# All low parts of the mixing stages' weights on VectorE

## The chip, the cores and the metric

The kernel runs on one core of one Trainium2 chip. The metric is the device time of one execution in microseconds (us); lower is better. The kernel before took 2455.51 us, the median of 3 runs (2453.41 to 2462.34).

## The reference

Two transformer blocks one after the other on x, 512 tokens of 1024 features in float32. What matters here is the order of the stages and which weights each multiplies:

```python
def hybrid_layer(...):                                  # first block
    x = x + 0.5 * swiglu_ffn(rmsnorm(x, ffn1_norm_g), ffn1_w_in, ffn1_w_out)
    h = rmsnorm(x, mix_norm_g)
    # h @ w_in -> q, k, v, conv and gates; block attention + gated convolution + memory attention
    x = x + (g_nsa * o_nsa + g_conv * o_conv + g_mem * o_mem) @ w_out
    x = x + 0.5 * swiglu_ffn(rmsnorm(x, ffn2_norm_g), ffn2_w_in, ffn2_w_out)

def second_block(...):
    x = x + _mixer_block(_rms(x, norm_mix_w), w_in, ...)  # windowed attention + gated linear attention
    x = x + _memory_xattn(_rms(x, norm_mem_q_w), _rms(mem, norm_mem_kv_w), ...)
    x = x + _swiglu(_rms(x, norm_ffn_w), w_gate, w_up, w_down)
    return _rms(x, norm_final_w)
```

Every `@` with a weight is a float32 product that the kernel makes of three products of shorter numbers.

## The kernel before

The stages follow each other: feed-forward f1, mixing stage `mix1`, feed-forward f2, mixing stage `mix2` with the memory attention `xattn` behind it, feed-forward f3. x is kept transposed, as 8 tiles of 128 features x 512 tokens.

A number is split into a high part (rounded to the matmul's input type) and a low part (what the rounding left). `mm3` (L233) multiplies high by high, high by low and low by high, so each weight has to be there as a pair `wh`, `wl`. `w` (L268 on) makes the pair: a DMA brings 128x1024 raw numbers into a tile `wr` (three buffers), ScalarE rounds them (`copy`, the CAST of L260, into `wh`), and then one `tensor_tensor` subtracts `wh` from `wr` into `wl` (all of them carry L242, the line of the helper `tt`). `wh` and `wl` have three buffers each in the mixing stages, so a pair can be made while the two before it are in use or ready. Both inputs of the subtraction lie in SBUF.

Which engine subtracts is said by the list `self.wes`, through which `w` goes round by a running number. In the feed-forward stages it is `[nc.vector]`; before `mix1` and before `mix2` it is set to `[nc.gpsimd, nc.gpsimd, nc.vector]`, so there two of three low parts are made by GpSimd and one by VectorE. `xattn` follows `mix2` with the same list. The 199 weight tiles of `mix1`, `mix2` and `xattn` give 133 subtractions to GpSimd. Two halves in `setup` are on GpSimd by name (`split=True`) and have nothing to do with the list.

Besides that, GpSimd multiplies and adds 128x512 tiles in the mixing stages (`cv`, `x`: L242 as well): 40 instructions. VectorE has most of what else is neither matmul nor activation: it evacuates each 512-column product from PSUM (`chunk` returns to a `mul` or `stt` by the caller), makes the low parts of activations (`split`, `stack`), the minima and scalings of the softmaxes, the recurrence `st` of the linear attention and the square roots (`rsqrt`). Some of these instructions read PSUM and one tile of SBUF, some read two tiles of SBUF: in `softmax_mem` the small `nm<-nm,mr4y` (128x1), in `nsa_v` the low part `vt<-vtmp,vt`, in `gla` the gate `og<-sq,og`, in `rsqrt` all its steps.

The code sets the order of the calls, but the framework sorts each engine's instructions by its own estimate of when they can start and puts in all waits; on the chip each engine then works its list off in that order. A low part made on VectorE therefore stands at some place of VectorE's list that the code alone doesn't tell; on GpSimd it stands in a list of its own.

Of the kernel before, what the change touches and what calls it, by code (L numbers as in the profile page):

```python
# [204 lines left out]
class _Net:  # L205
# [1662 lines left out]
    def run(self):  # L1868
        nc, tc = self.nc, self.tc
        self.PSB = {"g": 3, "s": 2, "t": 2, "o": 1}  # L1870
        self.pi = 0
        self.todo = []
        self.pre = {}
        self.mid, self.half = None, 3
        self.wes = [nc.vector]
        with ExitStack() as es:
            self.g = es.enter_context(tc.tile_pool(name="glob", bufs=1))
            self.wps = [(es.enter_context(tc.tile_pool(name="wts", bufs=1)), WC, 3)]
            self.wi = self.wk = 0
            self.pp = es.enter_context(tc.tile_pool(name="psum", bufs=1, space=bass.MemoryType.PSUM))  # L1880
            dp = es.enter_context(tc.tile_pool(name="dram", bufs=1, space=bass.MemoryType.DRAM))
            self.xd = dp.tile([KT, P, S], F32, name="xd")
            self.drel = dp.tile([16, LINE], F32, name="drel")
            self.dcmp = dp.tile([16, 1024], F32, name="dcmp")
            self.setup()
            self.gl5 = self.t(self.g, [P, 2], F32, "gl5", 1)
            o = _OFF["glan"]
            self.ts(self.gl5, self.cols[:, o:o + 2], 0.5, ALU.mult)
            self.oneb = self.ones[:, 0:1]

            def step(key, spill, late=False):
                self.begin_norm(key)

                def hook(n):
                    if spill:
                        self.spill(n)
                    self.norm_x(n)
                    if not late:
                        self.norm_sq(n)

                self.hook = hook
                return hook

            def done(tag):
                if tag in self.dbg:
                    for j in range(KT):
                        nc.sync.dma_start(self.dbg[tag][j], self.X[j])

            self.xq = es.enter_context(self.pool("xq", "right"))
            self.open_u()  # L1910
            step("ffn1", False)
            for j in range(KT):
                self.norm_x(j)
            for j in range(KT):
                self.norm_sq(j)
            self.end_norm()

            self.mem = {}

            def memory():  # L1920
                self.memkeep, self.memtmp = ExitStack(), ExitStack()
                keep = self.memkeep.enter_context(self.pool("memkeep", "right"))
                tmp = self.memtmp.enter_context(self.pool("memtmp", "right"))
                prep = self.mem_prep(tmp, keep, "mem1", "memn", self.mem, True)
                tabs = self.tables(tmp)
                self.todo = prep[:9] + tabs[:1] + prep[9:] + tabs[1:]

            self.ffn("f1", 0.5, self.deferred(step, "mix", True), 3, memory)
            self.memtmp.close()
            self.upool.__exit__(None, None, None)  # L1930
            done("d_f1")
            self.end_norm()
            self.pending("ffn2", False, step)
            self.wes = [nc.gpsimd, nc.gpsimd, nc.vector]
            self.mix1()
            self.wes = [nc.vector]
            done("d_m1")
            self.end_norm()
            self.ffn("f2", 0.5, self.deferred(step, "mix2", True), 3)
            self.upool.__exit__(None, None, None)  # L1940
            done("d_f2")
            self.end_norm()
            self.pending("mq2", False, step)
            self.wes = [nc.gpsimd, nc.gpsimd, nc.vector]
            self.mix2()
            done("d_m2")
            self.end_norm()
            self.pending("ffn3", False, step, True)
            self.xattn()
            self.xpool.__exit__(None, None, None)  # L1950
            self.wes = [nc.vector]
            done("d_x2")
            self.end_norm()
            self.open_u()
            self.ffn("f3", 1.0, None, 3)
            self.upool.__exit__(None, None, None)
# [33 lines left out]
```

## Time and profile before

| what | before |
|---|---|
| median of 3 runs | 2455.51 us (2453.41 to 2462.34) |
| the profiled execution | 2457.26 us; its span, first to last instruction, 2455.5 us |
| TensorE (PE) busy | 2365.4 us, 96% of the span |
| weight loads (PEld) busy | 2048.3 us, 83% |
| VectorE (DVE) busy | 1710.2 us, 70% |
| ScalarE (ACT) busy | 1160.2 us, 47% |
| GpSimd (POOL) busy | 431.6 us, 18% |
| low parts on GpSimd (`wl`) | 135 instructions, 317.2 us |
| low parts on VectorE (`wl<-wr,wh`) | 270 instructions, 326.5 us |

An engine's busy time is what it executes, waiting included where an instruction has started and can't go on; idle time has a releaser, the work whose end let the engine go on. PEclk is the granted clock of TensorE, 1.00 for 2.4 GHz and 0.50 for 1.2 GHz. The stages lie about so: f1 to 340 us, `mix1` 340 to 1140, f2 to 1480, `mix2` and `xattn` 1480 to 2060, f3 to the end.

### The profile page before, as it was taken

How to read it: one execution, taken by the hardware profiler on the slowest of the kernel's cores; microseconds unless marked ns; L12 is line 12 of the kernel's file. 1: busy time of each engine (PE TensorE's matmuls, PEld its weight loads, DVE VectorE, ACT ScalarE, POOL GpSimd, SP SyncE). 2: the span in 40 equal slices, each digit the busy share in tenths (PEclk: the TensorE clock that was granted, in tenths of full speed). 3: DMA queues.
4: the chain of work that ended last, by engine and by line, in shares of the span. 5: the costliest groups of instructions: out<-in, count | busy, mean ns of one | idle time of the engine just before them, and what ended most of it. 6: DMA issues, size and time to landing. Idle time of an engine off the chain costs nothing.

```text
span 2455.5 us, 35462 instructions
## 1 busy us (share of the span) xinstructions
PE 2365.4 (96%) x13618; PEld 2048.3 (83%) x13618; DVE 1710.2 (70%) x3150; ACT 1160.2 (47%) x2084; POOL 431.6 (18%) x260
## 2 busy tenths in 40 slices
PE   8999999899999999999999999998999998999997
PEld 7999978687788788877989898797888886889897
DVE  7766876865668666876767675558875367867675
ACT  6534443343445544545535353554665346644353
POOL 0000014331222222231000002121122331000000
PEclk9999999999999999999999999999999998999999
DMA  6645544231222122224445453122222331555551
GB/s 191 176 129 159 148 143 151 85 113 53 74 69 73 58 87 69 69 65 163 127 153 148 140 144 122 52 86 63 69 69 71 122 125 60 150 155 142 160 141 57
DMA packets 91318, 272.14 MB, mean 111 GB/s; under 512 B 10775, under 2 KB 19001, under 8 KB 91020
## 3 DMA queue, kind: packets, MB, share of 16 engines
q1 hardware_dynamic: 82748, 239.81, 29.7%
q0 software_dynamic: 8400, 30.06, 6.8%
q8 instruction: 107, 1.75, 0.3%
q14 instruction: 63, 0.52, 0.1%
HBM read 263.44 MB, written 6.40 MB: 110 GB/s over the span
## 4 chain that ended last, share of the span: by engine, by line
PE 63%; DVE 11%; ACT 2%; issue 2%; DMA 1%; POOL 0%; DVEq 0%; ACTq 0%; POOLq 0%
PE g L231 36%; PE s L231 12%; PE t L231 10%; PE o L231 3%; PE t L239 2%; DVE wl L242 2%; ACT wh L260 1%; DVE qk L242 1%; DMA wr<-f_s 1%; DVE sp L1259 0%; DMA wr<-f_o 0%; DVE cv L254 0%; DVE o L254 0%; POOL wl L242 0%; DVE xs L242 0%
## 5 line engine op out<-in xcount | busy, mean ns | idle before, releaser
L231 PE MATMUL g<-xs,wh 128*128 128x512 f32 (+1 forms) x3064 | 900.6, 376 | 7.4 <-ACT wh L260 3.0
L260 ACT CAST wh<-wr 128x1024 fp32r<-128x1024 f32 (+6 forms) x405 | 410.3, 1016 | 574.8 <-PE g L231 219.8
L231 PEld LDWEIGHTS g<-xs,wh 128*128 128x128 f32 x3064 | 555.1, 192 | 100.1 <-ACT wh L260 3.5
L231 PE MATMUL g<-xs,wl 128*128 128x512 f32 (+1 forms) x1532 | 573.2, 374 | 6.3 <-POOL wl L242 3.6
L242 POOL TENSOR_TENSOR wl<-wr,wh 128x1024 fp32r<-128x1024 f32 (+4 forms) x135 | 317.2, 2351 | 862.3 <-ACT wh L260 684.9
L242 DVE TENSOR_TENSOR wl<-wr,wh 128x1024 fp32r<-128x1024 f32 (+6 forms) x270 | 326.5, 1211 | 69.9 <-ACT wh L260 67.4
L231 PEld LDWEIGHTS g<-xs,wl 128*128 128x128 f32 x1532 | 293.2, 191 | 58.6 <-POOL wl L242 4.9
L231 PE MATMUL s<-xs,wh 128*128 128x256 f32 (+1 forms) x876 | 219.0, 339 | 1.4 <-ACT wh L260 1.4
L231 PE MATMUL t<-xs,wh 128*128 128x512 f32 (+1 forms) x860 | 213.2, 337 | 0.1
L555 POOL DMA_DIRECT2D wr<-f_s x57 | 49.1, 861 | 849.2 <-DMA wr<-f_s 202.3
L231 PEld LDWEIGHTS s<-xs,wh 128*128 128x128 f32 x876 | 150.5, 189 | 20.8 <-ACT wh L260 2.6
L231 PEld LDWEIGHTS t<-xs,wh 128*128 128x128 f32 x860 | 147.8, 189 | 18.1 <-DVE xs L242 0.5
L231 PE MATMUL t<-xs,wl 128*128 128x512 f32 (+1 forms) x430 | 145.4, 338 | 3.7 <-DVE wl L242 3.7
L231 PE MATMUL s<-xs,wl 128*128 128x256 f32 (+1 forms) x438 | 148.2, 338 | 0.0
L257 ACT ACTIVATE sp<-sp,nm 128x128 f32<-128x128 f32 x192 | 101.9, 532 | 55.2 <-DVE nm L1259 42.4
L242 DVE TENSOR_TENSOR ptl<-t,pth 128x512 fp32r<-128x512 f32 (+1 forms) x128 | 73.5, 603 | 55.5 <-ACT pth L260 55.1
L260 ACT CAST pth<-t 128x512 fp32r<-128x512 f32 (+1 forms) x128 | 62.1, 520 | 92.7 <-PE t L239 92.1
L231 PEld LDWEIGHTS t<-xs,wl 128*128 128x128 f32 x430 | 81.2, 189 | 13.1 <-DVE wl L242 4.5
L231 PEld LDWEIGHTS s<-xs,wl 128*128 128x128 f32 x438 | 82.9, 189 | 9.0
L231 PE MATMUL g<-th,wl 128*128 128x256 f32 x292 | 82.7, 283 | 1.5 <-DVE wl L242 1.0
L231 PE MATMUL g<-tl,wh 128*128 128x256 f32 x292 | 81.5, 279 | 0.0
L231 PE MATMUL g<-th,wh 128*128 128x256 f32 x292 | 81.5, 279 | 0.0
(521 smaller groups left out, 4820.0 us busy)
## 6 DMA issues: line engine op xcount, KB each, us to landing
wr<-f_ab SPq DMA_DIRECT2D x73, 512.0 KB, 3.8
wr<-f_s SPq DMA_DIRECT2D x57, 512.0 KB, 4.8
wr<-f_s POOLq DMA_DIRECT2D x57, 512.0 KB, 6.8
wr<-f_o SPq DMA_DIRECT2D x48, 448.0 KB, 3.8
wr<-m_f SPq DMA_DIRECT2D x40, 512.0 KB, 3.7
wr<-m_o SPq DMA_DIRECT2D x40, 512.0 KB, 3.5
w<-f_ab SPq DMA_DIRECT2D x57, 256.0 KB, 4.2
wr<-f_o SPq DMA_DIRECT2D x24, 512.0 KB, 4.7
```

Of the source, the lines that this page charges most:

```text
L231: self.pm = self.nc.tensor.matmul(o, l, r, start=first, stop=last, skip_group_check=more)
L239: self.nc.tensor.transpose(o, i, self.ident)
L242: (e or self.nc.vector).tensor_tensor(o, x, y, op=op)
L257: return self.nc.scalar.activation(o, x, f, **k)
L260: return self.nc.scalar.copy(o, x)
L555: nc.gpsimd.dma_start(rs, a[key + "_s"][c][:, D:], accum_op=ALU.add)
```

## The change

Before both mixing stages the list of engines for the low parts is one engine long, VectorE. The 133 subtractions that GpSimd did there go to VectorE; the roundings, the DMAs, the buffers and the matmuls are the same, and so are the 40 other GpSimd instructions and the two halves in `setup`.

```diff
             self.pending("ffn2", False, step)
-            self.wes = [nc.gpsimd, nc.gpsimd, nc.vector]
+            self.wes = [nc.vector]
             self.mix1()
             self.wes = [nc.vector]
             done("d_m1")
...
             self.pending("mq2", False, step)
-            self.wes = [nc.gpsimd, nc.gpsimd, nc.vector]
+            self.wes = [nc.vector]
             self.mix2()
```

## Rows read from the trace of the kernel before

**Rows 1.** Busy time by stage: us, busy (instructions) per engine, clock, DMA.
```profile
340.00:1140.00 800.00, 762.69 (x3881) 626.52 (x3880) 570.54 (x1188) 358.60 (x717) 224.83 (x111) 0.97 0.27 87
1140.00:1480.00 340.00, 337.71 (x2262) 309.85 (x2261) 243.72 (x376) 160.97 (x236) 18.84 (x20) 1.00 0.50 142
1480.00:2060.00 580.00, 563.03 (x2817) 470.74 (x2815) 369.66 (x729) 287.17 (x588) 147.71 (x81) 0.99 0.26 87
```

**Rows 2.** The same for instructions with `wl` alone: PE, PEld, DVE, POOL.
```profile
340.00:1140.00 800.00, 322.61 (x852) 164.52 (x852) 53.73 (x41) 178.70 (x75) 0.97 0.27 87
1480.00:2060.00 580.00, 266.54 (x698) 132.23 (x697) 36.28 (x29) 133.46 (x57) 0.99 0.26 87
```

**Rows 3.** Durations by tile: ns min/median/max, first and last start, shapes.
```profile
L242 POOL TENSOR_TENSOR wl<-wr,wh x135: 1277/2397/3245, 9.4 to 2048.6; 128x1024 fp32r<-128x1024 f32 x117, 128x768 fp32r<-128x768 f32 x6, 128x560 fp32r<-128x560 f32 x5, 128x912 fp32r<-128x912 f32 x5
L242 DVE TENSOR_TENSOR wl<-ws,wh x57: 1215/1225/1226, 47.9 to 2385.0; 128x1024 fp32r<-128x1024 f32 x57
L242 DVE TENSOR_TENSOR nm<-nm,mr4y x16: 152/159/2158, 544.9 to 608.3; 128x1 f32<-128x1 f32 x16
```

**Rows 4.** Timeline near 563 us, by engine: start, us, instruction, [idle before <-releaser].
```profile
563.31 2.16 DVE L242 TENSOR_TENSOR nm<-nm,mr4y 128x1 f32<-128x1 f32 x1
...
563.08 2.37 POOL L242 TENSOR_TENSOR wl<-wr,wh 128x1024 fp32r<-128x1024 f32 x1 [16.26 <-ACT wh L260]
...
566.21 0.38 PE L231 MATMUL s<-kmh,qh 128*128 128x256 f32 x1 [1.75 <-ACT pm L257]
```

**Rows 5.** Timeline near 892 us.
```profile
891.79 2.30 DVE L242 TENSOR_TENSOR vt<-vtmp,vt 128x256 fp32r<-128x256 f32 x1 [0.47 <-ACT vt L260]
...
891.46 2.34 POOL L242 TENSOR_TENSOR wl<-wr,wh 128x1024 fp32r<-128x1024 f32 x1 [2.51 <-ACT wh L260]
...
894.82 0.70 PE L239 MATMUL t<-ident,tabc 128*128 128x128 f32 x4 [3.75 <-DVE tabc L242]
```

**Rows 6.** Timeline: first and last of 89 lengthened VectorE groups, x2 of both.
```profile
345.30 3.03 DVE L254 SCALAR_TENSOR_TENSOR ml<-mraw,cols,mh 128x256 fp32r<-128x256 f32 x2
...
2046.38 2.83 DVE L242 TENSOR_TENSOR q<-qr,q 64x512 fp32r<-64x512 f32 x2
```

**Rows 7.** TensorE's waits in 340 to 1140 us: total us, times, longest.
```profile
PE g L231 <- DVE wl L242: 4.8, 2, 2.7
PE t L239 <- DVE tabc L242: 4.1, 3, 3.7
PE s L231 <- ACT pm L257: 3.9, 3, 1.7
PE g L231 <- POOL wl L242: 3.6, 3, 1.7
...
PE o L231 <- DVE rsl L242: 2.4, 2, 1.8
```

**Rows 8.** TensorE's waits in 1480 to 2060 us.
```profile
PE t L231 <- DVE stl L242: 5.5, 5, 1.5
PE t L239 <- DVE x L249: 2.5, 1, 2.5
PE o L231 <- ACT rsh L260: 2.0, 1, 2.0
```

**Rows 9.** Granted clock (0.50, after PEld, DVE, ACT, POOL) right behind rows 5.
```profile
895.30:898.70 3.40, 3.40 (x12) 2.92 (x11) 3.18 (x11) 2.25 (x8) 0.00 (x0) 0.50 0.42 161
```

**Rows 10.** Chain that ended last, 340 to 1140 us: shares of the 800 us.
```profile
by line: PE g L231 39.6%; PE s L231 6.4%; PE o L231 6.3%; PE t L239 5.3%; PE t L231 3.7%; DVE qk L242 1.9%; DVE sp L1259 1.4%; DVE wl L242 1.3%; issue 1.2%; DVE cv L254 1.1%; DVE o L254 0.9%; DVE nm L242 0.8%; ACT wh L260 0.8%; DVE vt L242 
```

**Rows 11.** VectorE's idle time before its `wl`, 1480 to 2060 us, and times.
```profile
  ACT wh L260: 32.4, 12
```

**Rows 12.** Timelines near 461 us: a run of VectorE work, TensorE's wait.
```profile
460.52 1.23 DVE L242 TENSOR_TENSOR wl<-wr,wh 128x1024 fp32r<-128x1024 f32 x1
...
461.80 0.79 PE L231 MATMUL g<-xs,wl 128*128 128x512 f32 x1 [2.69 <-DVE wl L242]
...
467.50 5.10 DVE L242 TENSOR_TENSOR zr<-kcr,pe 64x256 f32<-64x256 f32 x5
```

## The prediction

> **What bounds the kernel now.** I read the busy time by stage first [rows 1]. TensorE is idle for 800 - 762.7 = 37.3 us of `mix1` and 580 - 563.0 = 17.0 us of `mix2` with `xattn`; in f2, where VectorE makes every low part already, it is idle for 2.3 of 340 us. So TensorE bounds all stages, and what can be won in the mixing stages is those 54 us and the time lost to a lower clock (mean 0.97 and 0.99, which is 24 and 6 us of full-clock work). VectorE is busy for 71% and 64% of the two stages, as in f2 (72%): it is not the bound on average, but it feeds TensorE.
>
> Then TensorE's waits by releaser [rows 7, 8]. Hardly any names a low part made by GpSimd (3.6 us). Most name VectorE, or ScalarE directly behind VectorE, and the timelines at those places show one pattern. At 563 us VectorE's `nm<-nm,mr4y`, which works on one column and mostly takes 0.16 us [rows 3], takes 2.16 us; GpSimd's subtraction started 0.23 us earlier and ends at 565.45, and the small instruction ends 0.02 us later; the matmul behind it waited 1.75 us [rows 4]. At 892 us `vt<-vtmp,vt` takes 2.30 us for 256 columns, where VectorE's subtraction of 1024 takes 1.22 [rows 3]; it ends 0.29 us behind GpSimd's, and TensorE waited 3.75 us in all, a second held one having run a little earlier [rows 5]. All lengthened instructions have two inputs in SBUF. There are 89 of them beside a low part on GpSimd between 340 and 2060 us (the first and last are in the two groups of [rows 6]); their durations less those of the same instruction without GpSimd beside it sum to 140 us: 83 in `mix1`, 55 behind it, 2 between.
>
> **Removed.** 133 subtractions leave GpSimd (75 and 57 in the two stages [rows 2], one between), and with them 312 us of its time. GpSimd isn't on the path but for the 3.6 us, so its own time is worth little. What is worth something is VectorE's 140 us. The 40 other GpSimd instructions stay, and what they lengthen (10 us in 12 cases) stays with them.
>
> How much of that does TensorE feel? I go through its waits and give each the smaller of its length and of the lengthening just ahead of it. `mix1`: `pm` 3.9 (three times the `nm` case), `tabc` 3.5 of 4.1, `rsl` 2.4, VectorE's own `wl` 2.1 of 4.8 (one of its two was itself held): 11.9 us [rows 7]. `mix2`: `stl` 5.2 of 5.5 (behind a held gate or query instruction), `x` 2.1 of 2.5 (one held square-root step), `rsh` 2.0 (the same): 9.3 us [rows 8]. A dozen others of 0.3 to 2.0 us each give 10, as far as all of them together stay under the 54 us of idle time [rows 1]. Sum 31 us. Where one is lifted, ScalarE's link or the next evacuation is late next; I keep four fifths, 25 us, with 15 (half) and 31 as ends.
>
> The waits for a GpSimd `wl` (3.6 us) are for an instruction of 2.40 us that becomes one of 1.22 us [rows 3]: 1.8 us, ends 0 and 3.6.
>
> **Clock.** Behind such waits the granted clock falls to 0.50 (1.2 GHz) for a while: right behind the 3.75 us wait it is 0.50 for 3.4 us [rows 9]. I find six such stretches, from 366 to 2028 us, directly behind a wait of the list above, 34 us long together, in which 17 us of full-clock work were lost. Some have other waits beside them that stay: I take 8 us, ends 0 and 17.
>
> **Added.** VectorE gets 117 subtractions of 1024 columns at 1.225 us [rows 3], 143 us, and 16 narrower ones which, scaled by columns, make about 14: 158 us. It gives up 138 in the two stages, so its load there goes from 940 to some 960 of 1380 us [rows 1], 68 to 70%. It doesn't saturate. Were nothing lifted it would be 1098 us, 80%.
>
> What a subtraction costs depends on where it stands in VectorE's list, which the trace of before doesn't show for the 133. Two bounds. Below: nothing, if it falls into VectorE's idle 30%; a pair can be made two weight tiles ahead, so its own lateness has slack. A gain beyond the lifted waits is excluded, since the work is added. Above: the full 1.22 us whenever VectorE is on the path. The nearest rows are VectorE's own subtractions in the same stages: in `mix1` they hold 1.3% of the chain, 10.4 us [rows 10], of which 2.1 was the held one, so 8.3 us for 41, 0.20 each. In `mix2` they lie under the lines that the chain's row shows, 1.2 us for 29. 76 x 0.20 + 57 x 0.04 = 17.5 us on the chain. Some 41 us of VectorE's lengthening lay on the chain and came to the 31 us at TensorE, so I take three quarters of the 17.5 and a little for the fuller queue: +15 us, ends 0 and 38 (the whole of the compression's price below).
>
> One new wait: the subtraction waits at the head of VectorE's list for ScalarE's cast, with all evacuations queued behind it. VectorE's own 29 in `mix2` idled 32.4 us so, 12 times [rows 11], and no wait of TensorE there names them [rows 8]; I put it into the 15.
>
> **Sum.** -25 - 1.8 - 8 + 15 = -20 us, against the profiled execution's 2457.3 us: 2437.5. That execution lies 1.8 us over the median of the runs, so 2436 as a median.
>
> **Rivals.** (a) The delay is only exchanged. The subtraction can start where it starts today, when the cast is done; if it then stands ahead of the same `nm`, `vt` or `og`, it holds them for 1.22 us. 158 us come, 138 go, and the waits grow in that ratio, 31 x 158 / 138 = 35.5: with the 1.8 us back, 2455 + 2.7 = 2458; if the clock stretches shorten somewhat, 2450. For it: today's GpSimd subtractions are released by the same casts. Against it: the framework can put a VectorE subtraction behind a short instruction that is ready, and the 70 already there cost 0.20 and 0.04 us, not 1.22.
>
> (b) Slower: low parts come late in the compression of `mix1`. There VectorE runs `zr` for 5.10 us in one piece, and a subtraction on VectorE behind three `zr` has made TensorE wait 2.69 us [rows 12]. Between 450 and 550 us GpSimd makes 14 low parts. At 2.7 us each that is 38 us; the other 119 at 0.12 each (4.8 us for 41 [rows 2, 7]) make 14. With 25 + 2 + 8 lifted: 2455 + 17 = 2472. It decides from the point where a moved subtraction costs TensorE more than 35 / 133 = 0.26 us on average. For it: the run of 5.10 us. Against: 20 of the 140 us of lengthening lie between 450 and 550 us, and go. The Trainium skill, "Perfetto Trace Analysis", Optimizing Scalar/DVE Operations, says that where VectorE is saturated, handing work to ScalarE or even GpSimd may make sense. By that rule alone the change undoes a sensible split and (b) would hold. The same place adds that moving work between those two might not help since they share a read port of SBUF, and the held instructions of [rows 4, 5] agree with this second half.
>
> (c) It changes nothing, because few instructions move: excluded by the list's length, as all 199 tiles take its one entry.
>
> **Chances.** Forecast (2424 to 2446) 0.60, (a) (2442 to 2464) 0.26, (b) (2460 to 2490) 0.14. A measurement here tells about 0.5% from no change, 12.3 us, which is under 2443.2 or over 2467.8. Of the forecast 0.55 lies below 2443, 0.05 above; of (a) 0.02 is faster, 0.23 same, 0.01 slower, since it rests on a ratio; of (b) 0.02 same, 0.12 slower. So faster 0.57, same 0.30, slower 0.13. The range leaves out a tenth at each side: 2418 (the sum with 31 lifted, 3.6 for the late low parts, 8 for the clock and 3 added comes to 2416) to 2471 (the foot of (b)).
>
> **What would show it.** Right: VectorE's `nm<-nm,mr4y` has its longest under 0.5 us, `vt`, `og`, `qgl` and the square-root steps likewise; GpSimd's busy time falls to about 120 us; VectorE's stays within 30 us of 1710; TensorE's waits on `pm`, `tabc`, `stl`, `rsh` shrink to under half, and its idle time in the two stages from 54 to some 40 us or less; fewer stretches at 1.2 GHz. Wrong by (a): the same waits, now behind a 1.22 us `wl` on VectorE. Wrong by (b): waits `g <- DVE wl` of 2 us and more between 440 and 530 us. Wrong altogether would be VectorE's instructions still held to 2.4 us, by the 40 that stay.

## The result: 2398.8 us, and the profile after

| | before | after |
|---|---|---|
| median of the runs shown | 2455.59 us | 2398.80 us (2397.29 to 2403.09) |
| ratio to before, 95% interval | | 0.9767 [0.9748, 0.9785] |
| profiled execution | 2457.26 us | 2403.09 us |
| its span | 2455.5 us | 2401.0 us |
| mean granted clock | 0.980 | 0.989 |
| VectorE busy | 1710.2 us | 1720.8 us |
| GpSimd busy | 431.6 us | 119.8 us |

The change gains 57 us by the medians and 54 us between the two profiled executions. The forecast was 20 us, the fast end of its range 2418. So the direction was right, and the gain lies 19 us outside the range.

The busy time by stage, the first three columns being the stretch, its length and TensorE's busy time, then TensorE's weight loads, VectorE, ScalarE, GpSimd, clock and DMA. The stretches begin and end at the same TensorE instructions as those of [rows 1], to within a few of them:

```profile
340.00:1100.00 760.00, 747.28 (x3876) 615.43 (x3875) 566.27 (x1260) 357.32 (x715) 47.24 (x36) 0.99 0.29 91
1100.00:1440.00 340.00, 338.08 (x2263) 310.28 (x2262) 243.39 (x377) 161.03 (x236) 17.92 (x24) 1.00 0.51 142
1440.00:2006.00 566.00, 559.71 (x2819) 467.26 (x2817) 385.01 (x790) 287.76 (x591) 14.31 (x19) 1.00 0.28 89
```

Against [rows 1], `mix1` went from 800 to 760 us and `mix2` with `xattn` from 580 to 566: 40 and 14 us, the whole 54. The stage between them, f2, kept its 340. TensorE's idle time fell from 37.3 to 12.7 us and from 17.0 to 6.3, together from 54.3 to 19.0. The clock's mean rose from 0.97 and 0.99 to 0.99 and 1.00. Before, the records hold eight stretches at 1.2 GHz in `mix1`, 44 us long; after, these two parts of 6.8 us each (the second begins at 1070 us), of which this is the first:

```profile
507.00:513.80 6.80, 6.80 (x22) 5.53 (x22) 3.24 (x14) 1.14 (x2) 0.00 (x0) 0.50 0.21 72
```

In the second part there were two, 13.6 us long, and a third began 0.8 us before its end; after, one is left, which begins 4 us before the end. So 58.8 us at 1.2 GHz became 17.6, eleven stretches became three, and half of the difference, some 20 us, is full-clock work won back. Idle time gives 35 us and the clock 20, together the 54 us to within 2 us.

The instructions that make or read `wl` alone, same columns:

```profile
340.00:1100.00 760.00, 318.42 (x850) 161.16 (x851) 138.25 (x116) 0.00 (x0) 0.99 0.29 91
1440.00:2006.00 566.00, 264.90 (x698) 131.01 (x697) 109.23 (x86) 0.00 (x0) 1.00 0.28 89
```

Where [rows 2] has 41 and 29 subtractions on VectorE and 75 and 57 on GpSimd, all 116 and 86 are now on VectorE. VectorE got 84.5 + 73.0 = 158 us of work, as forecast, and yet is busy for 566 us as against 571 in `mix1` and 385 as against 370 behind it. The rest was time in which its instructions had been held. That is seen in their durations (ns, least, median and greatest):

```profile
L242 DVE TENSOR_TENSOR nm<-nm,mr4y x16: 151/159/161, 525.4 to 583.6; 128x1 f32<-128x1 f32 x16
L242 DVE TENSOR_TENSOR vt<-vtmp,vt x8: 411/418/426, 622.5 to 861.8; 128x256 fp32r<-128x256 f32 x8
```

`nm<-nm,mr4y` had a longest of 2158 ns [rows 3] and the `vt` of [rows 5] took 2.30 us. Now the longest of each is within 2% of its median. TensorE's waits in 340 to 1100 us (total, times, longest), for [rows 7]:

```profile
PE g L231 <- DVE wl L242: 3.1, 3, 1.5
PE t L239 <- DVE sp L249: 2.4, 6, 0.8
PE g L231 <- ACT xs L260: 2.0, 1, 2.0
PE o L231 <- DVE ptl L242: 1.6, 3, 0.6
...
PE s L231 <- DVE nm L1259: 0.7, 4, 0.2
PE t L239 <- DVE tabc L242: 0.4, 2, 0.2
```

`pm` and `rsl` have gone, `tabc` has 0.4 of its 4.1 us left, and `wl` on VectorE 3.1 of 4.8, though it is now made 116 times instead of 41. In `mix2`, for [rows 8]:

```profile
PE s L231 <- ACT pm L257: 1.2, 3, 0.7
PE t L239 <- DVE pm L249: 1.1, 1, 1.1
PE o L231 <- ACT pth L260: 0.7, 1, 0.7
PE o L231 <- ACT rsh L260: 0.5, 1, 0.5
```

Here `stl` (5.5 us) and `x` (2.5) are gone, and no wait names a weight's low part.

### The profile page after: what moved, and what is told of

Same layout as the page of the kernel before. It is cut to its first block, busy times and chain, and to the rows that moved or that the text cites. A ratio compares the mean times of both kernels' runs of the same rounds, so it can differ in the third digit from the quotient of the medians.

```text
span 2401.0 us, 35435 instructions
## 1 busy us (share of the span) xinstructions
PE 2348.8 (98%) x13618; PEld 2035.0 (85%) x13618; DVE 1720.8 (72%) x3283; ACT 1159.7 (48%) x2084; POOL 119.8 (5%) x127
## 4 chain that ended last, share of the span: by engine, by line
PE 65%; DVE 9%; DMA 2%; ACT 2%; issue 1%; DVEq 0%; ACTq 0%; POOLq 0%; SPq 0%
PE g L231 37%; PE s L231 12%; PE t L231 10%; PE o L231 3%; DVE wl L242 3%; PE t L239 3%; DMA wr<-f_s 1%; ACT wh L260 1%; DVE qk L242 1%; DMA wr<-f_o 1%; DVE ptl L242 0%; DVE sp L1259 0%; DVE q L242 0%; DVE cv L254 0%; DVE sp L1712 0%
## 5 line engine op out<-in xcount | busy, mean ns | idle before, releaser
L231 PE MATMUL g<-xs,wh 128*128 128x512 f32 (+1 forms) x3064 | 889.8, 372 | 4.0 <-ACT xs L260 2.0
L231 PEld LDWEIGHTS g<-xs,wh 128*128 128x128 f32 x3064 | 549.3, 189 | 92.8 <-ACT xs L260 2.4
L242 DVE TENSOR_TENSOR wl<-wr,wh 128x1024 fp32r<-128x1024 f32 (+6 forms) x403 | 485.1, 1205 | 94.0 <-ACT wh L260 88.5
L231 PEld LDWEIGHTS t<-xs,wh 128*128 128x128 f32 x860 | 147.6, 189 | 17.6 <-ACT e L260 0.2
L260 ACT CAST wh<-ws 128x1024 fp32r<-128x1024 f32 x57 | 59.8, 1049 | 44.2 <-PE g L231 20.1
```

What stands on the lines that cost most here:

```text
L231: self.pm = self.nc.tensor.matmul(o, l, r, start=first, stop=last, skip_group_check=more)
L242: (e or self.nc.vector).tensor_tensor(o, x, y, op=op)
L260: return self.nc.scalar.copy(o, x)
```

## The experiments

The question was no longer whether, but why so much more than 20 us. Three theories: the held instructions were worth more than their rows summed to (H); the change gave a better order of instructions (O); or the low parts came too late from GpSimd's 2.4 us instructions (L). Of the added work the question was whether it costs 15 us. `mixing`, where it stands in an edit, is a flag that is true in `mix1` and `mix2`; with `wi % 3 < 2` it picks the 133 tiles that the change moves. `w` subtracts at two places, the second for 10 of the 133 tiles; an edit that is shown at one stands at both, if nothing else is said. Times over after are differences of medians from different sessions, in which the kernel before took 2453 to 2456 us.

An instruction counts as lengthened below when it runs beside one of GpSimd's and takes over 15% and 0.1 us more than the median of the same instruction without one beside it.

**Putting GpSimd back, with nothing to do.** The kernel after, where GpSimd repeats the 133 subtractions into the raw tile, which nobody reads:

```
             self.tt(l[:, s], raw[:, s], h[:, s].bitcast(F32), ALU.subtract, e)
+            if self.mixing and self.wi % 3 < 2:
+                self.tt(raw[:, s], raw[:, s], h[:, s].bitcast(F32), ALU.subtract, nc.gpsimd)
```

> The kernel after the change, and for the same two of three weight tiles of the mixing stages GpSimd does the subtraction a second time, behind VectorE's, into the raw tile, which nobody reads any more. All low parts still come from VectorE, no matmul waits for GpSimd. Theory (GpSimd's two-input subtraction holds up VectorE instructions with two SBUF inputs): the 2 us long small VectorE instructions come back, 100 to 140 us of them, and the time rises from 2399 to 2440 to 2480 us, at or over the kernel before. Rival 1 (the gain comes from the low parts being ready 1.2 us earlier and from VectorE not having to share a list with nothing): low parts stay early, 2399 to 2410 us. Rival 2 (the gain comes from another order that the framework found): the extra work changes the order little, 2395 to 2410 us, and the long small instructions are there but cost nothing.

Measured: 2510.9 us, 1.024 [1.0214, 1.0266] of before, 112 us over after, with TensorE's instructions in the order of after but for two. No low part comes from GpSimd here. The small instruction of [rows 4] is back at its 2 us (start, duration, instruction, in brackets the idle time ahead and what ended it):

```profile
578.07 2.03 DVE L242 TENSOR_TENSOR nm<-nm,mr4y 128x1 f32<-128x1 f32 x1
...
577.71 2.37 POOL L242 TENSOR_TENSOR wr<-wr,wh 128x1024 f32<-128x1024 f32 x1 [14.58 <-DVE nm L242]
...
580.84 0.38 PE L231 MATMUL s<-kmh,qh 128*128 128x256 f32 x1 [1.42 <-ACT pm L257]
```

GpSimd's instruction ends at 580.08, the held one at 580.10, and the matmul waits for `pm` behind it, as before. The two parts by busy time:

```profile
340.00:1170.00 830.00, 772.34 (x3876) 630.88 (x3875) 663.62 (x1256) 357.00 (x710) 233.18 (x111) 0.96 0.26 83
1510.00:2112.00 602.00, 571.52 (x2814) 475.32 (x2813) 434.43 (x786) 287.58 (x587) 157.61 (x81) 0.97 0.26 83
```

TensorE idles 57.7 + 30.5 = 88 us, and the clock's mean is 0.96 and 0.97. VectorE is busy for 1098 of 1432 us, 77%: with the 158 us of work and the holds both on it. H is shown as a cause. The time is 31 us over the range that the theory gave, and the 133 cost twice what they cost before (112 and 57). A part of that may not be the holds: the raw tile stays taken longer, so the next load starts later. The next run bounds it. Another part is who is held. GpSimd's subtractions stand at other places here, and 44 of the 171 us of lengthening fall on 26 `TENSOR_SCALAR`s, which have one input; before it was 2 us on two of them. TensorE's longest sum of waits in 340 to 1170 us is behind such instructions:

```profile
PE t L239 <- DVE sp L249: 11.2, 10, 2.3
```

**GpSimd busy, but writing only.** The kernel after, with two `memset`s of the raw tile where the repeated subtraction stood:

```
+            if self.mixing and self.wi % 3 < 2:
+                for _ in range(2):
+                    nc.gpsimd.memset(raw, 0.0)
```

> The kernel after the change, and GpSimd writes zeros twice into the raw tile of the same 133 weight tiles once VectorE has made the low part. GpSimd is about as busy as before the change and its instructions sit at about the same places, but they read nothing from SBUF. If it is GpSimd's reading that holds VectorE up: no lengthened VectorE instructions, 2397 to 2408 us. If any GpSimd work beside VectorE does it, or if the raw tiles' later release does: 2420 to 2470 us.

Measured: 2415.3 us, 0.9844 [0.9829, 0.9858], 16.5 over after, between the two cases expected. GpSimd takes the raw tile for 256 us here (266 `memset`s, 20 of them at the second place), three quarters of the 332 us that the repeated subtractions took, so little of the 112 us can come from the tile being taken. The rows by duration:

```profile
L303 POOL MEMSET wr<- x246: 945/955/1183, 352.9 to 2008.9; 128x1024 f32 x123
L242 DVE TENSOR_TENSOR nm<-nm,mr4y x16: 153/159/161, 526.9 to 585.1; 128x1 f32<-128x1 f32 x16
L249 DVE TENSOR_SCALAR sp<-sp,sm x192: 270/402/1381, 633.5 to 1838.8; 128x256 f32<-128x256 f32 x80, 128x128 f32<-128x128 f32 x48, 128x384 f32<-128x384 f32 x32, 128x512 f32<-128x512 f32 x32
```

Of 188 instructions with two inputs in SBUF beside a `memset` five were lengthened, 3.7 us in all, and three of the five had one of GpSimd's 40 adds and products beside them too. But of 68 `TENSOR_SCALAR` from SBUF to SBUF, with one input, 63 were, 37 us in all, and the median of `sp<-sp,sm` rose from 348 to 402 ns. One place shows it, four of them that take 2.46 us beside two `memset`s; undisturbed, the four take some 1.1 (270 ns each):

```profile
723.63 2.46 DVE L249 TENSOR_SCALAR sp<-sp,sm 128x128 f32<-128x128 f32 x4
...
723.41 2.07 POOL L303 MEMSET wr<- 128x1024 f32 x2 [3.42 <-ACT sp L257]
```

So a GpSimd that reads nothing spares the two-input instructions and holds others. The Trainium skill, "SBUF — State Buffer", Who interferes with whom, parts the cases in this way: two SBUF inputs meet only a GpSimd instruction that reads SBUF, while copies, casts and `tensor_scalar` in a two-port mode meet any. The counts above, 5 of 188 and 63 of 68, agree with both halves, though the trace doesn't name the mode of an instruction.

The run settles one more rival, that a busy GpSimd by itself lowers TensorE's clock. GpSimd is busy for 314 us of the two parts, after for 62, and the clock's mean is the same (0.99 and 1.00):

```profile
340.00:1110.00 770.00, 749.88 (x3875) 614.84 (x3874) 586.77 (x1260) 357.14 (x715) 190.76 (x186) 0.99 0.29 90
1450.00:2015.00 565.00, 558.12 (x2813) 465.82 (x2811) 388.68 (x784) 285.73 (x581) 123.42 (x138) 1.00 0.28 89
```

**The same holds, in shorter pieces.** The kernel before, with 123 of the 133 GpSimd subtractions cut in four (the 10 at the second place stay whole). The same engine makes the same low parts, and nothing moves:

```
-            self.tt(l[:, s], raw[:, s], h[:, s].bitcast(F32), ALU.subtract, e)
+            n4 = 4 if e is nc.gpsimd and not split else 1
+            w4 = (s.stop - s.start) // n4
+            for q in range(n4):
+                s4 = slice(s.start + q * w4, s.start + (q + 1) * w4)
+                self.tt(l[:, s4], raw[:, s4], h[:, s4].bitcast(F32), ALU.subtract, e)
```

> The kernel before, with each of GpSimd's subtractions in the mixing stages cut into four of 256 columns; which engine makes which low part stays as before. Theory (a held VectorE instruction waits to the end of the one GpSimd instruction that is under way): most holds fall from some 2 us to under 0.7 us, though one may be caught by the next piece, and the time falls to 2415 to 2435 us. If the hold lasts as long as GpSimd has such work at all, or if GpSimd's being slow was the trouble: 2450 to 2465 us. If the hold is shared out evenly per element, whatever the pieces: 2450 us too.

Measured: 2424.2 us, 0.987 [0.9841, 0.9899]: 31 us won, though GpSimd is longer at its low parts than before (416 us, before 317). TensorE and VectorE run their instructions in exactly the order of the kernel before. By durations:

```profile
L242 POOL TENSOR_TENSOR wl<-wr,wh x504: 591/742/2628, 9.7 to 2024.6; 128x256 fp32r<-128x256 f32 x155, 128x192 fp32r<-128x192 f32 x8, 128x560 fp32r<-128x560 f32 x2, 128x912 fp32r<-128x912 f32 x2
L242 DVE TENSOR_TENSOR nm<-nm,mr4y x16: 151/160/529, 537.0 to 595.7; 128x1 f32<-128x1 f32 x16
```

A held instruction now waits for a piece of 0.74 us instead of one of 2.40: the longest `nm` falls from 2158 [rows 3] to 529 ns, and the sum of VectorE's lengthening, counted as in the prediction, from 140 to 67 us. The busy time:

```profile
340.00:1118.00 778.00, 755.99 (x3890) 621.82 (x3889) 526.78 (x1190) 359.84 (x720) 280.86 (x321) 0.98 0.28 89
1458.00:2035.00 577.00, 564.36 (x2819) 471.51 (x2819) 348.63 (x736) 288.70 (x593) 188.63 (x237) 0.99 0.27 87
```

TensorE's idle time is 22.0 + 12.6 = 34.6 us. This run speaks against O, because the order is the same, and against L, because GpSimd's work as a whole takes longer. (In the change itself TensorE's order differs in some 1200 of 13618 instructions; what that alone is worth isn't known.) Halving the lengthening gave a little over half of the gain: 31 / 73 = 0.42 us per us of lengthening. At that rate the whole 140 are worth 59 us, near what the change gave. The rate isn't a constant. Counted over all of GpSimd's instructions, VectorE's lengthening is 148 us before, 76 here, 17 after, 57 beside the `memset`s and 171 with the subtractions put back: 0.43 us here and 0.42 beside the `memset`s, but 112 / 154 = 0.73 where VectorE has the moved work as well.

**Part by part.** The kernel before, with the one list entry changed ahead of `mix1` alone, ahead of `mix2` alone, and (the second form) for half the moved tiles in both:

```
-            self.wes = [nc.gpsimd, nc.gpsimd, nc.vector]
+            self.wes = [nc.vector]
...
-            self.wes = [nc.gpsimd, nc.gpsimd, nc.vector]
+            self.wes = [nc.gpsimd, nc.vector, nc.vector]
```

> The kernel before with the change made for the first mixing stage alone. In the traces of before and after, the part of the time line from about 286 to 1126 us became 40 us shorter. If the parts add up: 2455 - 40 = 2415 us. If the gain is a matter of the whole order that the framework found: anything else, such as 2400 or 2440 us.

> The kernel before with the change made for the second mixing stage and the memory attention alone. In the traces the part from 1497 to 2125 us became 14.5 us shorter. If the parts add up: 2455 - 15 = 2440 us, and the gains of the two one-sided kernels sum to the 57 us of both.

> The kernel before with one of three low parts on GpSimd in the mixing stages in place of two. If each hold costs the same: half of the 57 us, 2427 us. If the lower clock multiplies the cost where holds lie close together: less than half is left, 2412 to 2422 us.

Measured: 2419.2 us (0.9849 [0.9814, 0.9883], 36 won), 2439.5 (0.9929 [0.9904, 0.9954], 15.5 won) and 2423.0 (0.9865 [0.9839, 0.9891], 32 won). The first two sum to 51 of the 57, and the parts of `mix1` and `mix2` stand as 36 to 15.5 (2.3 to 1), between the 83 to 55 us of lengthening (1.5 to 1) and the 40 to 14 of the windows (2.9 to 1). Half the tiles give 32 of 57, between the two cases expected and, with an interval of 6 us to each side, not apart from either. The gain is spread over both stages and over the tiles; no single place makes it.

**What the added work costs.** The kernel after with the 133 subtractions left out: the low parts of those tiles aren't made, and the matmuls read the high part in their place (`none` is true for these tiles, and their `l` is `h`).

```
-            self.tt(l[:, s], raw[:, s], h[:, s].bitcast(F32), ALU.subtract, e)
+            if not none:
+                self.tt(l[:, s], raw[:, s], h[:, s].bitcast(F32), ALU.subtract, e)
```

> The 133 subtractions are left out on any engine: the matmuls of these weight tiles read the high part twice, as many matmuls of the same shapes as before. It measures the held work alone, with nothing added to VectorE. If the moved subtractions cost next to nothing on VectorE: 2392 to 2400 us, so the whole gain of 57 us is what GpSimd took. If they cost the 15 us of the prediction: 2380 to 2386 us, and GpSimd took some 72.

Measured: 2397.8 us, 0.9769 [0.9752, 0.9787], one us under after. By stretches:

```profile
340.00:1094.00 754.00, 744.14 (x3877) 613.75 (x3876) 485.85 (x1184) 356.19 (x715) 46.14 (x36) 1.00 0.30 92
1434.00:2003.00 569.00, 564.22 (x2828) 474.39 (x2826) 319.40 (x736) 286.34 (x595) 13.26 (x19) 0.98 0.28 88
...
1526.70:1540.40 13.70, 13.70 (x43) 10.12 (x43) 6.26 (x13) 5.34 (x12) 0.00 (x0) 0.50 0.01 1
```

VectorE has 146 us less to do, and TensorE idles 9.9 + 4.8 = 14.7 us, as against 19.0 after. `mix1` is 6 us shorter than after. `mix2` is 3 us longer, since one stretch runs at 1.2 GHz which in the kernel after has the full clock, and half of its 13.7 us is lost. In all the two parts run at 1.2 GHz for 25.8 us here and for 17.6 after, so 4 us more of full-clock work are lost. With the clock equal the work left out is thus worth 4 us by idle time and 3 + 4 = 7 us by the length of the parts; by the time it is worth 1. TensorE's order differs here (fewer dependences, so the framework places work otherwise), so the parts can be laid against those of after only roughly, and whether the lost clock belongs to that order isn't known.

The kernel after with a second set of the 133 subtractions on VectorE, into the raw tile, and with every second of them (`wi % 3 == 0`):

```
+            if self.mixing and self.wi % 3 < 2:
+                self.tt(raw[:, s], raw[:, s], h[:, s].bitcast(F32), ALU.subtract, nc.vector)
```

> The kernel after the change, and VectorE does the same 133 subtractions a second time, into the raw tile. It measures what the added VectorE work costs: 158 us more, its load in the mixing stages from some 70% to 82%. If an added subtraction costs what the prediction took (0.11 us at TensorE): 2414 us. If it falls into idle time as the result suggests: 2399 to 2406 us. If VectorE is near its bound, as the slower rival had it: 2430 us and more.

> As the kernel with the 133 doubled VectorE subtractions (27 us slower than the change), but only 67 of them are doubled. If an added subtraction has one price at these loads (0.2 us): 2399 + 13 = 2412 us. If VectorE's idle time swallows the first ones and the price comes only as it fills up: 2399 to 2405 us.

Measured: 2426.2 us (0.9888 [0.9873, 0.9902]), 27.4 over after, and 2411.6 (0.9815 [0.9789, 0.984]), 12.8 over: 0.21 and 0.19 us each. The full set lies between two of the cases expected, above the 2414 us of the prediction's price; the half set is where one price puts it, to within an interval of some 6 us. The windows of the full set:

```profile
340.00:1127.00 787.00, 757.43 (x3871) 622.87 (x3870) 644.27 (x1334) 358.39 (x715) 51.82 (x36) 0.98 0.28 88
1467.00:2030.00 563.00, 558.19 (x2813) 467.77 (x2811) 441.24 (x840) 285.35 (x582) 14.31 (x19) 0.99 0.28 88
```

`mix1` is 27 us longer than after and `mix2` 3 us shorter. Of the 27, 12 lie between 379 and 510 us (times of the kernel after), where the compression is. There TensorE's waits name the subtractions:

```profile
PE g L231 <- DVE wl L242: 6.6, 4, 4.3
PE g L231 <- DVE kcr L242: 4.3, 1, 4.3
```

So nearly half of what a second set of subtractions costs falls at the place that rival (b) named; the first set didn't pay there.

**One step further.** The kernel after with the 40 other element-wise GpSimd instructions of the mixing stages on VectorE too:

```
-            self.mul(u, u, cg, nc.gpsimd)
+            self.mul(u, u, cg)
...
-        self.tt(self.M[c], self.M[c], o, ALU.add, self.nc.gpsimd)
+        self.tt(self.M[c], self.M[c], o, ALU.add)
```

> The kernel after the change, and GpSimd's 40 other element-wise instructions of the mixing stages on VectorE too (0.69 us each there, 28 us in all), so that nothing on GpSimd can hold VectorE. The holds that remain after the change sum to about 17 us. If half of that reached TensorE and the added work costs 0.1 us an instruction: 2394 us. If the added work stands in VectorE's way like the doubled subtractions did (0.2 us each): 2400 us. Much worse (over 2410 us) would mean that GpSimd's adds relieved a chain that runs through VectorE.

Measured: 2400.6 us, 0.9772 [0.9748, 0.9796], the same as after. No VectorE instruction is lengthened any more (after, 17 us were), VectorE has 28 us of work more, and in the time the two cancel. No kernel of these beats the kernel after by more than its interval.

## Why the prediction was right in sign and too small

**The bound: right.** TensorE bounds the stages, and what could be won was its 54 us of idle time and its clock. The gain is 35 us of the one and 20 of the other.

**The mechanism: right.** It was VectorE's two-input instructions held by GpSimd's. Putting GpSimd's reads back brings the holds and more than the whole time back, shortening the pieces wins half of it with the order unchanged, and writing alone hardly holds those instructions. That all lengthened instructions have two inputs was nearly so: two `TENSOR_SCALAR`s with one, 2 us together, were lengthened as well.

**The term of the lifted waits: too small.** -25 us was 31 times four fifths, as something else would be late next. The fifth taken off is the step that failed first. The waits named one by one, those for a GpSimd `wl` among them, came to 28.8 us before and come to 4.0 after: 24.8 us lifted, where the list gave 11.9 + 9.3 + 1.8 = 23.0. All other idle time fell from 25.5 to 15.0 us, by 10.5, where the list gave 10. So the list at its full length, 33 us, was near the 35 us measured, with the added work in it, and nothing of size was late next: the waits of `mix1` left after hold 3.1 us at most by one releaser. In the run without the 133 on either engine TensorE idles 14.7 us, so lifting alone takes 54.3 - 14.7 = 39.6 us there. If its other order is let pass, the list missed some 7 us by giving each wait the smaller of its length and of the lengthening *just ahead* of it. A hold further back on VectorE's list, which is 70% full, can be passed on. The kernel before has such a place:

```profile
487.48 0.73 PE L231 MATMUL g<-xs,wh 128*128 128x512 f32 x2 [2.21 <-ACT wh L260]
```

ScalarE's cast stood behind an activation that waited for a VectorE instruction at 484.83 us. Ahead of that on VectorE's list, from 475.92 to 481.13 us, two instructions of 1.2 and 0.6 us, `zl` and `zr`, took 2.57 and 2.54 beside GpSimd's subtractions. After, no wait for `wh` is left in `mix1`. That this is the way all of the 7 us came about isn't shown.

By the quarters a us of lengthening was worth 0.42 us of time, clock included. The prediction's 25 + 8 over 140 is 0.24.

**The clock: too small.** -8 us was half of the 17 that six stretches directly behind a listed wait had lost; some 20 us came back. Followed by TensorE's instructions, eight of the eleven stretches went and three stayed: those at 527, 1110 and 2059 us are the ones at 507, 1070 and 2002 us after. Of the six that were counted five went, 27 us long, which is 14 us of full-clock work: taking half was the one mistake. The other was to count these six alone. Three more went, 17 us long and worth 8.5. The one at 462 us stood behind the late `wl` of [rows 12], the one at 489 behind the wait for `wh` above, and the one at 725 behind no wait of TensorE over 0.05 us; why it went isn't known. (The last stretch lies 3 us further inside the part after, which takes 1.6 off.) Which would stay could be told in part. The one at 1110 us is behind a wait for ScalarE's `xs`, 2.0 us before and after. The one at 527 us falls into 26 matmuls of four columns each, 3.4 us long, in both kernels, and after no wait of TensorE over 0.05 us stands in the 20 us ahead of it.

**The added work: too dear.** +15 us, with 0 and 38 as ends. By idle time it is 19.0 - 14.7 = 4.3 us, by the time of the run that leaves it out 1, by the length of the parts with the clock made equal 7. The price of 0.20 us each, taken from the share of VectorE's own `wl` in the chain [rows 10], is what a *further* set costs on top (0.19 and 0.21). In the chain of the kernel after, 340 to 1100 us, the lines hold these shares:

```profile
by line: PE g L231 44.1%; PE s L231 6.9%; PE o L231 6.6%; PE t L239 5.9%; PE t L231 4.1%; DVE qk L242 2.3%; DVE wl L242 1.8%; DVE sp L1259 1.5%; DVE cv L254 1.1%; issue 1.0%; ACT wh L260 0.8%; DVE ptl L242 0.7%; DMA wr<-m_f 0.6%; DVE sm L24
```

`wl` on VectorE is 1.8% of 760, 13.7 us for 116 instructions, 0.12 each: 3 us more than before for 75 more of them. A line's share of the chain divided by its count was the wrong price for more of the line: the 41 may have stood in the chain because holds had put them there, which no run parts. Why the first set costs nearly nothing and the second 27 us isn't settled; in the mixing parts VectorE's load is 72% after and 80% with the second set.

In sum, the idle term was to be -25 - 1.8 + 15 = -12 and is -35; the clock was to be -8 and is -20.

**The new wait: right.** The subtraction at the head of VectorE's list waits for the cast more often, here before `wl` in 1440 to 2006 us (idle us, times):

```profile
  ACT wh L260: 47.9, 41
```

It was 32.4 us in 12 cases [rows 11], and no wait of TensorE there names a weight's low part.

**The rivals.** (a), the delay only exchanged: against it stand the durations and the lifted waits. Why the subtraction, half as long on VectorE as the hold was on GpSimd, doesn't do the same harm, was only argued (the framework can put it behind a short instruction that is ready). (b), late low parts in the compression: the longest `g <- DVE wl` is 1.5 us where it asked for 2 us and more. Its place is real, as the second set shows, its price was not reached. (c) was excluded rightly.

**What would show it.** Each sign named for "right" is there: no `nm`, `vt` or square-root step over 0.5 us, `og` and `qgl` at no more than 0.69, their own median, GpSimd at 119.8 us, VectorE 11 us from 1710, the four waits under half, idle time at 19 where some 40 or less was asked, three stretches at 1.2 GHz instead of eleven. That idle time could come to 19 was in the text as "or less" and in no term of the sum.

## What to carry to other kernels

An engine that isn't the bound can still be the cause: look for instructions of VectorE that are far longer than their own median, and for the GpSimd instruction that they end with. Price such holds by the bound engine's waits at their full length and add the stretches at the lower clock behind them; take nothing off for what might be late next unless a row shows it. The sum of the lengthening over all instructions is a second way to the price: here 0.42 us of time came back per us of it, and where VectorE was fuller a us cost 0.73. If the work can't move, cutting it in pieces shortens each hold and won half.

## What the runs showed of the hardware that I had not expected

A GpSimd instruction that only writes holds VectorE's `TENSOR_SCALAR` from SBUF to SBUF (63 of 68, 37 us together), at 16.5 us of time for 266 `memset`s of 0.95 us. An instruction that is held counts as busy in the profile: VectorE took on 158 us of work, and its busy time grew by 11. And the clock gave back more than half as much as the idle time: 20 us beside 35, with eight of eleven stretches at 1.2 GHz gone.
